# A two-layer diffusion trunk on one core: the FFN's first product by seven block products, on single-bank PSUM tiles

## Chip, core and metric

The kernel runs on one core of a Trainium2 chip. The metric is device microseconds of one execution; three runs of the kernel before give a median of 2444.55 us (2443.7 to 2446.66).

## What is computed

640 tokens (512 latent and 128 context, 1024 wide) pass two layers. All arrays are float32.

```
x = x + g1 * mixers(rmsnorm(x) * (1 + sc1) + sh1)        # three attention branches, gates, output projection
h = rmsnorm(x) * (1 + sc2) + sh2
a, b = split(h @ w_ffn_in)                               # 1024 -> 2 x 2816
x = x + g2 * ((silu(a) * b) @ w_ffn_out)                 # 2816 -> 1024
sh1, sc1, g1, sh2, sc2, g2 = silu(c) @ w_mod + b_mod     # two conditioning vectors c
```

## The kernel before

Activations lie transposed, 128 channels on the partitions and the 640 tokens along the row, in two halves of 320 (`HALF`). For float32 accuracy each operand is a high part (`whi`, `h[:, 0]`) rounded to the matmul's format and a low part (`wlo`, `h[:, 1]`), and `group` (L420) issues three matmuls of 320 columns per 128x128 weight tile: high by high, high by low, low by high.

Weights come in chunks of 128 x 1024 float32, eight tiles each. `weights` loads a chunk to `raw` (two buffers, DMA queue of SP), ScalarE copies it to `whi` (`hi`), and POOL subtracts to `wlo` (`lo`; for attention chunks a DMA accumulates instead). There are four buffers of `whi` and of `wlo`.

The FFN has 22 inner tiles f of 128 channels, in two parts of 11 (`SEG`, `PARTS`). For each f and half `ffn_in` runs two products (gate and up, eight groups each) into one two-bank tile `S`, and `after` applies silu on ScalarE, multiplies on VectorE (`s<-s,S`), copies the high part on ScalarE and subtracts the low part on VectorE (`act<-s,act`). `ffn_out` then multiplies the part's tiles into eight output rows m, each with both halves in an `S` tile, and `residual` adds them to `x` on VectorE (`x<-S`). In the last part the final two rows are done first for one half and then for the other (`FO_SPLIT = 66`).

`mod_dve` makes the conditioning values on VectorE: pieces of `w_mod` (`mr`, 128x512) are multiplied with the two vectors silu(c), spread over all partitions in SBUF (`cb`), and summed along the row (L519, output `md`). In layer 0, 96 of these 320 operations run about the output projection and 224 in the FFN.

The order of all engines is made when the kernel is built: each piece of work is a generator with a priority, and `_Order.run` places the one that can start first by a table of costs (`dve`, `act`, `ptt`, `dma`). Dense products have priority 1000, weights 20, FFN finishing 40, `mod_dve` 200 (lower numbers go first). `MOD_SPREAD = 1.4` is the cost in us by which conditioning products are placed in the FFN. On the chip every engine runs its list in that order.

## Time and profile before

| | us |
|---|---|
| median of 3 runs | 2444.55 |
| profiled execution | 2444.26 |
| its span, first to last instruction | 2442.5 |
| TensorE busy | 2365.4 |
| VectorE busy | 1510.9 |
| ScalarE busy | 1195.5 |
| POOL busy | 773.6 |

The span is that of the profiled execution, and 1.8 us of its time lie around it. PE is TensorE, PEld its weight loads, DVE VectorE, ACT ScalarE. Instructions of helpers carry the helper's line: L311 is ScalarE's activation, L334 and L338 VectorE's two- and three-operand operations, L350 POOL's subtraction, L419 to L421 the three matmuls of a group.

### The profile page before, as it was taken

How to read it: one execution, taken by the hardware profiler on the slowest of the kernel's cores; microseconds unless marked ns; L12 is line 12 of the kernel's file. 1: busy time of each engine (PE TensorE's matmuls, PEld its weight loads, DVE VectorE, ACT ScalarE, POOL GpSimd, SP SyncE). 2: the span in 40 equal slices, each digit the busy share in tenths (PEclk: the TensorE clock that was granted, in tenths of full speed). 3: DMA queues.
4: the chain of work that ended last, by engine and by line, in shares of the span. 5: the costliest groups of instructions: out<-in, count | busy, mean ns of one | idle time of the engine just before them, and what ended most of it. 6: DMA issues, size and time to landing. Idle time of an engine off the chain costs nothing.

```text
span 2442.5 us, 44315 instructions
## 1 busy us (share of the span) xinstructions
PE 2365.4 (97%) x17084; PEld 2322.6 (95%) x17084; DVE 1510.9 (62%) x3621; ACT 1195.5 (49%) x2676; POOL 773.6 (32%) x694
## 2 busy tenths in 40 slices
...
GB/s 238 96 82 114 85 70 64 107 96 100 221 224 112 177 144 142 138 149 149 148 126 113 109 108 101 56 69 109 105 96 142 111 76 70 83 73 78 70 78 61
DMA packets 100579, 274.22 MB, mean 112 GB/s; under 512 B 11408, under 2 KB 25360, under 8 KB 100112
## 3 DMA queue, kind: packets, MB, share of 16 engines
...
## 4 chain that ended last, share of the span: by engine, by line
PE 77%; DVE 8%; issue 3%; DMA 2%; ACT 2%; POOL 1%; DVEq 0%; SPq 0%; POOLq 0%; ACTq 0%
PE S L420 13%; PE S L419 13%; PE S L421 13%; PE B L419 6%; PE B L421 6%; PE B L420 6%; PE B L1028 4%; PE B L722 2%; PE B L723 2%; PE B L724 2%; PE S L1000 2%; PE S L999 2%; PE B L1264 2%; PE B L1263 2%; DVE md L519 1%
## 5 line engine op out<-in xcount | busy, mean ns | idle before, releaser
L350 POOL TENSOR_TENSOR wlo<-raw,whi 128x1024 fp32r<-128x1024 f32 x158 | 390.2, 2471 | 694.1 <-ACT whi L311 693.8
L420 PE MATMUL S<-h,whi 128*128 128x320 f32 x1408 | 438.3, 311 | 6.7 <-DVE h L338 5.8
L419 PE MATMUL S<-h,whi 128*128 128x320 f32 x1408 | 438.2, 311 | 0.0
L421 PE MATMUL S<-h,wlo 128*128 128x320 f32 x1408 | 437.1, 310 | 0.0
L311 ACT ACTIVATE whi<-raw 128x1024 fp32r<-128x1024 f32 x268 | 282.7, 1055 | 282.4 <-PE S L420 229.2
L722 PE MATMUL B<-whi,h 128*128 128x256 f32 x928 | 274.3, 296 | 1.5 <-ACT nat L311 1.5
L420 PEld LDWEIGHTS S<-h,whi 128*128 128x128 f32 x1408 | 266.0, 189 | 9.7 <-DVE h L338 7.0
L723 PE MATMUL B<-wlo,h 128*128 128x256 f32 x928 | 263.2, 284 | 5.0 <-DMA wlo<-raw 5.0
L419 PEld LDWEIGHTS S<-h,whi 128*128 128x128 f32 x1408 | 266.1, 189 | 0.8 <-ACT h L311 0.4
L421 PEld LDWEIGHTS S<-h,wlo 128*128 128x128 f32 x1408 | 266.2, 189 | 0.0
L724 PE MATMUL B<-whi,h 128*128 128x256 f32 x928 | 263.4, 284 | 2.2 <-POOL h L350 2.2
L519 DVE SCALAR_TENSOR_TENSOR md<-mr,cb 128x512 f32<-128x512 f32 x320 | 247.0, 772 | 20.8 <-DMA mr<-wt 16.0
L419 PE MATMUL B<-h,whi 128*128 128x320 f32 x768 | 245.1, 319 | 0.2 <-ACT acc L311 0.2
L421 PE MATMUL B<-h,wlo 128*128 128x320 f32 x768 | 238.2, 310 | 0.7 <-DMA wlo<-raw 0.7
L420 PE MATMUL B<-h,whi 128*128 128x320 f32 x768 | 237.8, 310 | 0.0
L419 PE MATMUL S<-act,whi 128*128 128x320 f32 x704 | 218.0, 310 | 0.0
L421 PE MATMUL S<-act,wlo 128*128 128x320 f32 x704 | 217.5, 309 | 0.0
L420 PE MATMUL S<-act,whi 128*128 128x320 f32 x704 | 217.5, 309 | 0.0
L334 DVE TENSOR_TENSOR s<-s,S 128x320 f32<-128x320 f32 x88 | 42.9, 487 | 281.9 <-ACT s L311 281.8
L419 PE MATMUL B<-u,whi 128*128 128x320 f32 x640 | 202.5, 316 | 5.3 <-ACT u L311 4.2
L311 ACT ACTIVATE s<-S 128x320 f32<-128x320 f32 x88 | 38.5, 438 | 333.1 <-PE S L421 333.1
L311 ACT ACTIVATE P<-S,mx 128x768 f32<-128x768 f32 (+4 forms) x240 | 180.8, 756 | 41.8 <-DVE mx L1013 29.9
...
## 6 DMA issues: line engine op xcount, KB each, us to landing
...
mr<-wt SPq DMA_DIRECT2D x160, 256.0 KB, 3.1
...
```

Of the source, the lines that this page charges most:

```text
L311: fn = lambda: self.nc.scalar.activation(out, in_, func, **kw)
L350: return ("POOL", 0.147 + 0.0021 * _n(out), lambda: self.nc.gpsimd.tensor_tensor(out, a, b, op=op), 0.08)
L419: mm(out, lhsT=wh, rhs=xh, start=first, stop=False)
L420: mm(out, lhsT=wh, rhs=xl, start=False, stop=False)
L421: mm(out, lhsT=wl, rhs=xh, start=False, stop=last)
L519: yield ("DVE", each, lambda w=d["raw"], b=b, r=r: nc.vector.scalar_tensor_tensor(md, w, 1.0, b, op0=ALU.mult, op1=ALU.mult, accum_out=r), ...
L722: mm(d, lhsT=hh, rhs=wh, start=kt == 0, stop=False)
L723: mm(d, lhsT=hh, rhs=wl, start=False, stop=False)
L724: mm(d, lhsT=hl, rhs=wh, start=False, stop=kt == KT - 1)
L999: mm(o, lhsT=q, rhs=kh, start=True, stop=False)
L1000: mm(o, lhsT=q, rhs=kl, start=False, stop=True)
L1028: nc.tensor.transpose(t[:, i * P:(i + 1) * P], a, self.ident)
```

## The change

For inner tiles 3 to 21 (`PLAIN = 3`) the product [gate; up] = W h is taken as a 2 x 2 block product: gate and up are the block rows, the two halves of the 1024 input channels the inner blocks, the two token halves the block columns. Seven block products of four groups replace the eight.

- Inputs: `seven_inputs` makes once per layer, from `h`, four pairs of tiles `ht` (sums and differences of channel and token halves, again high and low). The sums are on VectorE, in `act` buffers.
- Weights: a tile's gate and up chunks come as one unit (`raw`, `raw2`); `sums` makes four 128x512 sums on VectorE (`ws`, and in place in `raw2`), and the unit is split in four high and low parts, three of 1024 and one of 512 columns.
- Outputs: `seven` sends each product to a bank, and `post` combines them with seven additions on VectorE (`fu`, `fv` and in the banks) and a copy on ScalarE. The multiplication with silu now writes into the bank, and the low part is taken from there (`hidden`).
- Banks: the FFN uses six single-bank tiles in turn, four `F` in the place of the `S` tiles and two of the `B` banks.
- Parts of 8, 8 and 6 inner tiles, so three rounds of `ffn_out` a layer.
- Conditioning: silu(c) lies in PSUM (in `S` about the output projection, in two `B` banks in the FFN, half of it at a time there, reloaded between), loaded in pieces through `cr`. `MOD_SPREAD` is 0.75, `mr` has four buffers throughout (before three, in the FFN eight), and the last four conditioning tiles of layer 1 move from layer 0's FFN to layer 1's, so 192 products are in layer 0's and 32 in layer 1's.

```diff
-WO_SPLIT, FO_SPLIT = 4, 66
-SEG = 11
+WO_SPLIT, FO_SPLIT = 4, 6
+SEG = 8
 PARTS = [range(a, min(a + SEG, NF)) for a in range(0, NF, SEG)]
+PLAIN = 3
...
-MOD_SOON, MOD_SPREAD = 0.7, 1.4
+MOD_SOON, MOD_SPREAD = 0.7, 0.75
...
+    def open_banks(self):
+        self.banks = [self.t("F", [P, 512])[:, 0:HALF] for _ in range(4)]
+        for _ in range(2):
+            self.banks.append((yield from self.get("D", [P, 512]))[:, 0:HALF])
...
+        def sums():
+            for c in todo:
+                if not c["seven"]:
+                    continue
+                yield self.wait(c["loaded2"])
+                ws = c["ws"] = yield from self.get("ws", [P, CH])
+                ra, rb = c["raw"], c["raw2"]
+                yield self.tt(ws[:, h1], rb[:, h1], rb[:, h2], ALU.add)
+                yield self.tt(ws[:, h2], ws[:, h1], ra[:, h1], ALU.subtract)
+                self.o.fire(c["s1"])
+                yield self.tt(rb[:, h1], ra[:, h1], rb[:, h1], ALU.subtract)
+                self.o.fire(c["s3"])
+                yield self.wait(c["lo_ok"][1])
+                yield self.tt(ws[:, h2], ra[:, h2], ws[:, h2], ALU.subtract)
+                self.rel("raw")
+                self.o.fire(c["s4"])
...
+                for n, e in enumerate(("loaded", "s1", "s4", "s3") if c["seven"] else ("loaded",)):
+                    yield ("acq", "whi")
+                    yield ("acq", "wlo")
+                    c["hi"].append(self.t("whi", [P, CH], F32R))
+                    c["lo"].append(self.t("wlo", [P, CH], F32R))
+                    yield self.wait(c[e])
+                    x, w = self.part(c, n)
+                    yield self.act(c["hi"][n][:, 0:w], x, AF.Copy)
...
+        n = 512 if home == "T" else D
...
+        def vectors():
+            for _ in range(2):
+                cv.append((yield from self.get(home, [P, n])))
+            used = None
+            for at, _, ok, done in plan:
+                if used is not None:
+                    yield self.wait(used)
+                for c in range(2):
+                    for i in range(2) if at is None else (at,):
+                        r = yield from self.get("cr", [P, 512])
+                        yield self.dma(r, self.I["cb"][:, c, i * 512:(i + 1) * 512], 128 * 4 * 512)
+                        to = 0 if at is not None else i * 512
+                        yield self.act(cv[c][:, to:to + 512], r, AF.Silu)
+                        self.rel("cr")
+                self.o.fire(ok)
+                used = done
...
+                        o = 0 if at is not None else i * 512
+                        b, r = cv[c][:, o:o + 512], a[:, q, c, i:i + 1]
+                        yield ("DVE", each, lambda w=d["raw"], b=b, r=r: nc.vector.scalar_tensor_tensor(
+                            md, w, 1.0, b, op0=ALU.mult, op1=ALU.mult, accum_out=r), 0.13)
...
-            yield self.tt(s, s, d[:, 1], ALU.mult)
-            self.rel("S")
-            yield self.act(act[f][:, 0, half], s, AF.Copy)
-            yield self.tt(act[f][:, 1, half], s, act[f][:, 0, half].bitcast(F32), ALU.subtract)
-            self.rel("s")
-            hit()
-        a, b = part[0], part[1]
-        steps = [(a, 0), (b, 0), (a, 1), (b, 1)] + [(f, half) for f in part[2:] for half in range(2)]
+            yield self.act(s, d[0], AF.Silu)
+            self.bank_done(d[0])
+            yield from self.hidden(s, d[1], act[f][:, :, half], hit)
...
+        for f in part:
+            if f >= PLAIN:
+                act[f] = yield from self.get("act", [P, 2, 2, HALF], F32R)
+                yield from self.seven(h, act[f], act_ok[f])
...
+    def seven_inputs(self, h, h_ok):
...
+            for kt in (k, k2):
+                for half in range(2):
+                    yield self.wait(h_ok[half][kt])
+            t = (yield from self.get("act", [P, 2, 2, HALF], F32R)).rearrange("p a b t -> p a (b t)").bitcast(F32)
+            x, y = t[:, 0], t[:, 1]
+            for kt, z in ((k, x), (k2, y)):
+                yield self.tt(z, h[kt][:, 0].bitcast(F32), h[kt][:, 1].bitcast(F32), ALU.add)
+            yield self.tt(x[:, a], x[:, b], x[:, a], ALU.subtract)
+            yield self.tt(x[:, b], y[:, b], x[:, b], ALU.subtract)
+            yield self.tt(y[:, b], y[:, b], x[:, a], ALU.subtract)
+            yield self.tt(y[:, a], y[:, a], y[:, b], ALU.subtract)
+            hits = self.counter(2, lambda k=k: (self.rel("act"), self.o.fire(self.ht_ok[k])))
...
+                yield self.act(d[:, 0], z, AF.Copy)
+                yield self.tt(d[:, 1], z, d[:, 0].bitcast(F32), ALU.subtract)
+                hits()
...
+    def seven(self, h, act, act_ok):
...
+        def post():
+            s_ok = [self.ev(), self.ev()]
+            yield self.wait(done[1])
+            v = yield from self.get("fv", [P, HALF])
+            yield self.act(v, p[1], AF.Copy)
+            self.bank_done(p[1])
+            yield self.wait(done[6])
+            u = yield from self.get("fu", [P, HALF])
+            yield add(u, p[6], v)
+            self.bank_done(p[6])
+            yield self.wait(done[2])
+            yield add(p[2], p[2], v)
+            o.spawn(gate(0, p[2], s_ok[0]), 39)
+            yield self.wait(done[5])
+            yield add(v, p[5], u)
+            yield self.wait(done[7])
+            yield add(u, p[7], u)
+            self.bank_done(p[7])
+            yield add(p[5], p[5], u)
+            yield self.wait(done[3])
+            yield add(p[3], p[3], v)
+            self.rel("fv")
+            o.spawn(gate(1, p[3], s_ok[1]), 39)
+            def second():
+                yield self.wait(s_ok[1])
+                yield from self.hidden(silu[1], p[5], act[:, :, 1], hit)
+            o.spawn(second(), 40)
+            yield self.wait(done[4])
+            yield add(p[4], p[4], u)
+            self.rel("fu")
+            yield self.wait(s_ok[0])
+            yield from self.hidden(silu[0], p[4], act[:, :, 0], hit)
+        o.spawn(post(), 40)
...
+        def go(i, part, col, xs):
+            p[i] = yield from self.bank()
+            yield self.wait(c["lo_ok"][part])
+            for k in range(n):
+                wh, wl = (t[part][:, col + k * P:col + (k + 1) * P] for t in (c["hi"], c["lo"]))
+                xh, xl = xs(k)
+                yield self.group(p[i], wh, wl, xh, xl, k == 0, k == n - 1)
+            o.fire(done[i])
+        two = lambda t, s: (t[:, 0, s], t[:, 1, s])
+        half = CH // 2
+        yield from go(1, 0, 0, lambda k: two(h[k], a))
+        for ok in self.ht_ok:
+            yield self.wait(ok)
+        yield from go(6, 1, half, lambda k: two(self.ht[k][1], b))
+        yield from go(2, 0, half, lambda k: two(h[n + k], a))
+        self.chunk_done()
+        yield from go(5, 1, 0, lambda k: two(self.ht[k][0], a))
+        self.chunk_done()
+        yield from go(7, 3, 0, lambda k: two(self.ht[k][0], b))
+        yield from go(3, 2, 0, lambda k: two(h[n + k], b))
+        self.chunk_done()
+        yield from go(4, 3, half, lambda k: two(self.ht[k][1], a))
+        self.chunk_done()
+    def hidden(self, s, d, out, hit):
+        yield self.tt(d, d, s, ALU.mult)
+        self.rel("s")
+        yield self.act(out[:, 0], d, AF.Copy)
+        yield self.tt(out[:, 1], d, out[:, 0].bitcast(F32), ALU.subtract)
+        self.bank_done(d)
+        hit()
...
-        split = FO_SPLIT if end else KT * n
+        split = (FO_SPLIT if end else KT) * n
...
-            mods = {"cb": 1, "md": 1, "ma": 2, "mr": 3}
+            mods = {"cr": 1, "md": 1, "ma": 1, "mr": 4}
...
-            fctx = self.pool("f", {"act": SEG, "s": 1})
+            self.scores_ctx.close()
+            pctx = self.pool("pf", {"F": 4}, space=PSUM)
+            fctx = self.pool("f", {"act": SEG, "s": 2, "ht": 8, "raw2": 2, "ws": 1, "fu": 1, "fv": 1})
             o.fire(f_open)
+            o.fire(self.f_ok[l])
+            o.spawn(self.seven_inputs(*h2), 12)
...
+            mctx = self.pool("m", mods)
+            here, ahead = [(l, j) for j in range(20, 24)], [(l + 1, j) for j in range(20)]
+            steps = [((0,), here), ((1,), here)]
             if not last:
-                mctx = self.pool("m", dict(mods, mr=8))
-                here = [(l, j) for j in range(20, 24)] if l == 0 else []
-                self.mod_dve(here + [(l + 1, j) for j in range(24)], 200, MOD_SPREAD)
+                steps += [((1,), ahead), ((0,), ahead)]
+            self.mod_dve(steps, 200, MOD_SPREAD, "T")
```

On VectorE, in layer 0's FFN while inner tiles are computed, the order before was as follows (`md` are conditioning products, `s` and `act` the finishing of inner tiles).

```order
L334 TENSOR_TENSOR act_10764<-s_10901,act_10764 128x320
L519 SCALAR_TENSOR_TENSOR md_10577,ma_10941<-mr_10703,cb_10502 128x512
L519 SCALAR_TENSOR_TENSOR md_10577,ma_10941<-mr_10727,cb_10502 128x512
L334 TENSOR_TENSOR s_10977<-s_10977,S_10905 128x320
L519 SCALAR_TENSOR_TENSOR md_10577,ma_10941<-mr_10727,cb_10502 128x512
L334 TENSOR_TENSOR act_10904<-s_10977,act_10904 128x320
```

At the same place it now reads (`ws` and the row with `raw` on the left are weight sums, `F` and `B` banks, `fu` and `fv` combinations):

```order
L359 TENSOR_TENSOR ws_10976<-raw_1997_10851 128x512
L359 TENSOR_TENSOR act_10817<-F_10285,act_10817 128x320
L359 TENSOR_TENSOR ws_10976<-ws_10976,raw_10773 128x512
L359 TENSOR_TENSOR act_10817<-B_10287,act_10817 128x320
L359 TENSOR_TENSOR raw_1997_10851<-raw_10773,raw_1997_10851 128x512
L359 TENSOR_TENSOR fu_11002<-F_10284,fv_10980 128x320
L617 SCALAR_TENSOR_TENSOR md_10508,ma_10509<-mr_10845,B_10505 128x512
L359 TENSOR_TENSOR B_10286<-B_10286,fv_10980 128x320
L617 SCALAR_TENSOR_TENSOR md_10508,ma_10509<-mr_10902,B_10504 128x512
L359 TENSOR_TENSOR fv_10980<-F_10282,fu_11002 128x320
```

The finishing and the conditioning products read a bank; the weight sums, which are new, stand between them with both inputs in SBUF.

On POOL, one inner tile's low parts were two of 1024 columns and are now these four (the fifth row begins the next tile):

```order
L375 TENSOR_TENSOR wlo_11019<-raw_10773,whi_11018 128x1024
L375 TENSOR_TENSOR wlo_11040<-ws_10976,whi_11039 128x1024
L375 TENSOR_TENSOR wlo_11079<-ws_10976,whi_11078 128x512
L375 TENSOR_TENSOR wlo_11111<-raw_1997_10851,whi_11110 128x1024
L375 TENSOR_TENSOR wlo_11163<-raw_10956,whi_11162 128x1024
```

The second and the third wait for weight sums of VectorE, and the fourth stands behind them.

On VectorE again, the end of layer 0's input transformation, before tile 3's second product (`act_10729` is the fourth pair's sums, `ht` the low parts of transformed inputs):

```order
L359 TENSOR_TENSOR act_10729<-h_10117 128x640
L359 TENSOR_TENSOR ht_10727<-act_10643,ht_10727 128x640
L359 TENSOR_TENSOR act_10729<-h_10121 128x640
L359 TENSOR_TENSOR ht_10728<-act_10643,ht_10728 128x640
L359 TENSOR_TENSOR act_10729<-act_10729 128x320
L359 TENSOR_TENSOR ws_10651<-raw_10603,ws_10651 128x512
L359 TENSOR_TENSOR act_10729<-act_10729 128x320
L359 TENSOR_TENSOR F_10285<-F_10285,s_10743 128x320
```

All of this is new there; weight sums and the finishing of the first three tiles stand among it.

## Rows read from the trace of the kernel before

**Rows 1.** The page, part 1: busy us, share of the span, instructions.
```profile
PE 2365.4 (97%) x17084; PEld 2322.6 (95%) x17084; DVE 1510.9 (62%) x3621; ACT 1195.5 (49%) x2676; POOL 773.6 (32%) x694
```
**Rows 2.** Windows, both FFNs: us, busy PE, PEld, DVE, ACT, POOL; clock, DMA, GB/s.
```profile
767.00:1242.00 475.00, 471.11 (x3183) 468.49 (x3181) 316.06 (x723) 134.70 (x215) 166.59 (x73) 0.99 0.43 145
1955.00:2430.00 475.00, 469.70 (x3165) 467.31 (x3165) 139.83 (x202) 124.19 (x202) 159.92 (x71) 0.99 0.20 71
```
**Rows 3.** Timeline of PE at the FFN's end: start, us, instruction.
```profile
2409.70 0.31 PE L419 MATMUL S<-act,whi 128*128 128x320 f32 x1
...
2419.38 0.31 PE L419 MATMUL S<-act,whi 128*128 128x320 f32 x1
```
**Rows 4.** Groups by form, DVE, layer 0's FFN (767 to 1242 us).
```profile
L519 DVE SCALAR_TENSOR_TENSOR md<-mr,cb 128x512 f32<-128x512 f32 x224 | 170.0, 759 | 3.6
L334 DVE TENSOR_TENSOR act<-s,act 128x320 fp32r<-128x320 f32 x44 | 66.0, 1500 | 4.6 <-ACT act L311 4.5
...
L338 DVE SCALAR_TENSOR_TENSOR x<-S,mo,x 128x320 f32<-128x320 f32 x16 | 8.8, 551 | 51.3 <-PE S L421 51.3
```
**Rows 5.** Tile views of s and md, whole run: ns min/median/max, starts.
```profile
L334 DVE TENSOR_TENSOR s<-s,S x88: 480/487/489, 784.0 to 2350.5; 128x320 f32<-128x320 f32 x88
...
L334 DVE TENSOR_TENSOR act<-s,act x88: 476/1470/2699, 788.7 to 2351.8; 128x320 fp32r<-128x320 f32 x88
...
L519 DVE SCALAR_TENSOR_TENSOR md<-mr,cb x320: 675/686/2935, 623.7 to 1227.6; 128x512 f32<-128x512 f32 x160
```
**Rows 6.** Timeline of DVE, layer 0's norm and FFN.
```profile
761.03 0.48 DVE L334 TENSOR_TENSOR ssq<-ssq,sq 128x320 f32<-128x320 f32 x1
761.43 0.55 DVE L338 SCALAR_TENSOR_TENSOR nu<-x,ac,ssq 128x320 f32<-128x320 f32 x1
...
805.87 2.51 DVE L334 TENSOR_TENSOR act<-s,act 128x320 fp32r<-128x320 f32 x1 [0.21 <-ACT act L311]
808.31 2.90 DVE L519 SCALAR_TENSOR_TENSOR md<-mr,cb 128x512 f32<-128x512 f32 x1
...
811.25 0.69 DVE L519 SCALAR_TENSOR_TENSOR md<-mr,cb 128x512 f32<-128x512 f32 x1
...
811.98 0.69 DVE L519 SCALAR_TENSOR_TENSOR md<-mr,cb 128x512 f32<-128x512 f32 x1
```
**Rows 7.** Timeline of POOL, start of layer 0's FFN.
```profile
794.58 2.41 POOL L350 TENSOR_TENSOR wlo<-raw,whi 128x1024 fp32r<-128x1024 f32 x1 [5.93 <-ACT whi L311]
...
805.61 5.04 POOL L350 TENSOR_TENSOR wlo<-raw,whi 128x1024 fp32r<-128x1024 f32 x2 [4.61 <-ACT whi L311]
815.70 2.76 POOL L350 TENSOR_TENSOR wlo<-raw,whi 128x1024 fp32r<-128x1024 f32 x1 [5.04 <-ACT whi L311]
```
**Rows 8.** Groups by form, POOL and ACT, layer 0's FFN.
```profile
L350 POOL TENSOR_TENSOR wlo<-raw,whi 128x1024 fp32r<-128x1024 f32 x64 | 160.7, 2512 | 272.8 <-ACT whi L311 272.7
...
L311 ACT ACTIVATE whi<-raw 128x1024 fp32r<-128x1024 f32 x67 | 70.8, 1056 | 124.0 <-PE S L420 116.0 <-issue 7.1 <-DMA raw<-w 1.0
```
**Rows 9.** Timeline of DVE: the norm's end, the third tile's end.
```profile
789.13 1.26 DVE L338 SCALAR_TENSOR_TENSOR h<-nu,mo,h 128x192 fp32r<-128x192 f32 x4
...
818.65 0.49 DVE L334 TENSOR_TENSOR s<-s,S 128x320 f32<-128x320 f32 x1 [0.17 <-ACT s L311]
```
**Rows 10.** Window after TensorE's wait at the start of layer 0's FFN.
```profile
776.00:780.00 4.00, 4.00 (x14) 3.38 (x13) 3.82 (x6) 1.00 (x2) 1.43 (x1) 0.50 0.39 134
```
**Rows 11.** Timeline of DVE and a window, end of layer 0's FFN.
```profile
1230.90 0.55 DVE L338 SCALAR_TENSOR_TENSOR x<-S,mo,x 128x320 f32<-128x320 f32 x1 [2.19 <-PE S L421]
...
1241.11 0.68 DVE L338 SCALAR_TENSOR_TENSOR x<-S,mo,x 128x192 f32<-128x192 f32 x2
...
1242.00:1246.00 4.00, 2.32 (x12) 1.64 (x11) 3.96 (x9) 2.61 (x6) 2.41 (x3) 1.00 0.82 205
```
**Rows 12.** Window and DVE group by form, layer 0's output projection (640 to 755, 767 us).
```profile
640.00:755.00 115.00, 104.57 (x683) 103.02 (x682) 99.04 (x259) 35.01 (x57) 25.65 (x14) 0.97 0.72 215
...
L519 DVE SCALAR_TENSOR_TENSOR md<-mr,cb 128x512 f32<-128x512 f32 x84 | 68.7, 818 | 13.2 <-DMA mr<-wt 12.2
```

207 lines of the change are left out of this document (138 added, 69 removed).

## Prediction, made before the change ran

> **What bounds the kernel now.** I read the page first: the span is 2442.5 us, and TensorE is busy for 97% of it, with its weight loads close behind; VectorE comes next at 62% [rows 1]. So the time is TensorE's work, and a change is worth what it takes off TensorE, less what it makes TensorE wait for. The windows then show where the change acts: the FFN runs from 767 to 1242 us in layer 0 and from 1955 to 2430 us in layer 1, TensorE is busy for 471 and 470 of the 475 us, at a granted clock of 0.99 [rows 2]. There is nearly no wait to win there; what can go is matmuls. In the timeline 22 groups of three FFN matmuls lie between 2409.70 and 2419.38 us [rows 3], which gives 9.68 / 66 = 0.1467 us per matmul (the 0.31 us of a row is its length in the pipe). In the same windows VectorE is at 316 us in layer 0 and 140 us in layer 1 [rows 2]: layer 0 carries 224 conditioning products (`md`) in its FFN [rows 4], layer 1 none.
>
> The next view is VectorE against POOL. An operation on VectorE with both inputs in SBUF is sometimes 0.48 us and sometimes 2.5: `act<-s,act` has a minimum of 476, a median of 1470 and a maximum of 2699 ns, while `s<-s,S`, the same shape with one input in PSUM, stays between 480 and 489 in all 88 cases [rows 5]. The timeline shows why: at 805.87 `act<-s,act` takes 2.51 us and at 808.31 an `md` takes 2.90, while POOL has two `wlo` of 2.5 us each from 805.61 on [rows 6, 7]. So POOL holds VectorE up for as long as its own instruction lasts, but only where VectorE reads two tensors from SBUF.
>
> The Trainium skill, page "SBUF — State Buffer", section "SBUF: two separate sides", says this as a rule: VectorE with two SBUF inputs and a GpSimd instruction that reads SBUF hold a shared port pair exclusively, and whichever starts second waits out the whole of the other. By that rule the trace agrees (2.51 against 0.48 us), and the rule speaks against this change, which adds such operations; rival C is what it comes to.
>
> **The change, part by part.** The sum is made against the profiled execution, 2444.3 us; the median of the three runs, 2444.55, is 0.3 us from it.
>
> Matmuls. An inner tile now takes 2 x 2 x 8 groups of three, 96 matmuls or 14.1 us. By seven products of four groups it is 84, or 12.3 us. The order shows 16706 rows on PE before and 16250 now, 456 fewer, which is 12 x 19 tiles x 2 layers. 456 x 0.1467 = **-66.9 us**, half of it in each layer. Everything else is what may be given back.
>
> VectorE inside a block tile. The order shows per tile four weight sums 512 wide with both inputs in SBUF, seven combinations and four finishing operations 320 wide with an input or output in PSUM, and in layer 0 about six conditioning products (some 115 of its 192 stand among the 19 block tiles). A 320-wide operation follows the next after 0.40 us (761.03 to 761.43), a conditioning product after 0.73 (811.25 to 811.98) [rows 6]; a 512-wide sum is then some 0.64 by its width. Layer 0: 4 x 0.64 + 11 x 0.40 + 6 x 0.73 = 11.4 us of the 12.3 us that TensorE has for the tile. It fits, with 0.9 us to spare, before any wait for POOL. Layer 1: 7.0 of 12.3.
>
> POOL has four low parts per tile, three of 1024 and one of 512 columns: 3 x 2.51 + 1.26 = 8.8 us of 12.3 [rows 8], so it is busy 72% of the time in which the sums must run. The conditioning products now read PSUM and are free of it. Bounds for the wait per tile: 0 if the sums fall into POOL's pauses; 4 x 1.0 = 4.0 us if each pays what `act<-s,act` pays on average (1500 ns in this window against a minimum of 476 [rows 4, 5]). I take 2.0: the first sum starts as POOL ends the short low part and begins the next long one, the last starts when POOL waits for it. 11.4 + 2.0 = 13.4 against 12.3, so VectorE is late by 1.1 us more on each tile, and since its order is fixed TensorE ends up waiting for banks and weights: 1.1 x 19 = **+20 us** in layer 0 (0 to 59). In layer 1 7.0 + 4.0 still fits; I put **+4** for single late sums (0 to 15).
>
> ScalarE has 3.5 x 1.056 us of high parts per tile [rows 8] and about 2.5 us more, some 6 of 12.3: covered. Banks: the product held longest is the fourth, from 7.0 us into the tile until its gated result is split, some 1.3 us into the next; by hand at most four of the six banks are held at once, so they cost nothing until VectorE is two products (3.5 us) behind. The weights' second part gets its buffers 7.0 us into the tile before, is split by about 11.4 (1.06 on ScalarE, POOL free from 9.0, 2.5 there) and used at 14.1, 2.7 us later. These two reserves are the cover; the lateness above eats them.
>
> Entry. The second product of tile 3 needs all transformed inputs. Before, the third tile ends at about 818 us (its `s<-s,S` at 818.65) and the norm's last write on VectorE at 790.4 [rows 9]; the tile's first product gives 1.8 us more, so the inputs are due at 819.7. From 790.4 VectorE has 16 operations 640 wide (0.80 by width) and 16 of 320, 9 finishing ones, 4 sums and 3 conditioning products: 12.8 + 6.4 + 3.6 + 2.6 + 2.2 = 27.6, less two that stand before the norm's end: 816.4. Nearly all of it reads two SBUF tensors, and five `wlo` lie between 794.58 and 818.46 [rows 7], 12.6 us in all. With half of them in the way: 822.7, a stall of 3 us, and after a stall TensorE shows the low clock for a while: 14 matmuls in 4 us at a granted 0.50 from 776 on [rows 10], that is 1.2 instead of 2.4 GHz. **+4 us** per layer, **+8** (0 to 24).
>
> Ends. The last two output rows are done by halves; with 6 inner tiles in the last part instead of 11 the first half's end lies 12 groups (5.3 us) ahead of the second's, not 22 (9.7; the rows show 1230.90 and 1241.11). The next layer's norm and the final one start 4.4 us later against TensorE's end. At 1242 TensorE is already half idle, 2.32 of 4 us [rows 11]. **+5 us** over both ends (0 to 10).
>
> Output projection of layer 0. Its conditioning products take 818 ns there against 675 at best [rows 5, 12], and TensorE idles 10 of 115 us with VectorE at 99 [rows 12]. Out of POOL's way they free 84 x 0.14 = 12 us of VectorE, but the DMAs are at 0.72 too, and they stay: **-2 us** (-8 to +4, as the vectors now come by four loads through one buffer).
>
> The third output part adds 16 residual additions a layer on VectorE, 0.55 us each [rows 4], in stretches with six conditioning products per 7 us; they fit, at nothing, and if VectorE is behind there they lengthen the 20 by up to 9.
>
> Sum: -66.9 + 20 + 4 + 8 + 5 - 2 = -31.9, so **2412 us**.
>
> **The rivals.**
> A, VectorE keeps up. The sums fall into POOL's pauses, the wait stays below the 0.9 us to spare, and only small losses stand: -66.9 + 2 (entry) + 2 + 4 - 2 = -61, 2383 us. For it: the finishing operations are moved off two SBUF inputs, and 72% is not all. Against it: 0.9 us is little, and every row class with two SBUF inputs shows waits.
>
> C, VectorE becomes the bound of layer 0 and the kernel is slower. Place: the sums and the entry; price: each sum waits 1.0 us, 11.4 + 4.0 = 15.4 against 12.3, 3.1 x 19 = 59; the entry meets all five low parts, 829 against 819.7, and 3 us of low clock, 24 for both layers; layer 1 15, ends 10: -66.9 + 108 = +41, 2485 us. It turns against the old kernel where the wait per tile passes 0.9 + (66.9 - 15) / 19 = 3.6 us. For it: after a POOL instruction the next one can begin before VectorE's (808.31 is such a row [rows 6]); against it: that needs all four sums to meet POOL every time.
>
> D, both cancel within 0.2%, about what a measurement of this kernel can tell from no change (5 us): a wait of 3.3 to 3.9 us per tile, 2439 to 2449 us.
>
> **How the numbers follow.** The forecast, a gain of which layer 0 gives most of its half back, 0.57; A 0.20; D 0.07; C 0.16. Faster is forecast and A, 0.77; same D, 0.07; slower C, 0.16. The likeliest time is 2412, its own range 2390 to 2439. For 8 in 10 the range reaches down to A's value, 2384, and up over D into the lower part of C, 2454.
>
> **What would show it.** Right: 456 fewer matmuls; layer 1's FFN shorter by 25 us or more, layer 0's by about 10; VectorE above 90% in layer 0's block tiles, sums with a mean of 1 us or more against 0.6, `md` near 690 ns without long ones; one TensorE wait of a few us in tile 3 of each layer. Wrong: if layer 0's FFN shrinks as much as layer 1's (A), if it is longer than 475 us (C), if TensorE's waits in block tiles end by DMA or ScalarE instead of VectorE, or if the entry stalls by over 12 us a layer.

## The result, and the profile after

The changed kernel takes 2433.44 us (median of 4 runs, 2430.18 to 2435.53) beside 2445.14 us for the kernel before in the same comparison: a ratio of 0.9947, 95% interval 0.9933 to 0.996. It is faster by 11.7 us, half a per cent; 32 were forecast. The profiled execution took 2430.18 us, its span is 2428.4 us, 14.1 us less than that of the profile before.

The page's first part and the windows of the two FFN stages, after (columns as in [rows 1, 2]):

```profile
PE 2318.7 (95%) x16628; PEld 2267.0 (93%) x16628; DVE 1783.1 (73%) x4151; ACT 1275.4 (53%) x2818; POOL 916.3 (38%) x770
```
```profile
762.00:1239.00 477.00, 447.07 (x2947) 437.82 (x2945) 430.85 (x909) 172.41 (x281) 236.63 (x111) 0.98 0.41 137
1958.00:2413.00 455.00, 442.09 (x2945) 437.68 (x2943) 298.87 (x535) 165.09 (x270) 234.01 (x108) 0.98 0.25 85
```

TensorE has 456 matmuls less, as forecast. Layer 1's FFN is 20 us shorter than in [rows 2]; layer 0's is as long as it was. There TensorE is idle for 30 of 477 us instead of 4 of 475, and VectorE is busy for 431 us instead of 316.

Where the time went, from the starts of the matmuls in the timeline. A tile's loss is the interval between its first matmul and the next tile's, less its number of matmuls x 0.1467 us; a stage is told from its first matmul to its last:

| us | before | after | difference |
|---|---|---|---|
| start of layer 0's FFN | 767.1 | 762.1 | -5.0 |
| layer 0's FFN | 473.6 | 476.5 | +2.9 |
| from one FFN to the other | 712.6 | 719.4 | +6.8 |
| layer 1's FFN | 474.3 | 454.4 | -19.9 |
| behind it, to the end of the span | 14.8 | 16.0 | +1.2 |

| loss after, us | layer 0 | layer 1 |
|---|---|---|
| inner tile 0 (before: 8.6, 9.3) | 10.0 | 8.2 |
| first block tile, 3 | 6.6 | 7.0 |
| end of part 0: tile 7 and its second product | 3.5 + 4.0 | 3.5 + 4.0 |
| parts 1 and 2 | 20.8 | 0 |
| last second product | 0.5 | 0.5 |

All other tiles run back to back. What I had not expected is the third row: the same 7.5 us in both layers, although layer 1 was to have VectorE time to spare.

VectorE's groups by form in layer 0's FFN (762 to 1239 us) show what changed there:

```profile
L617 DVE SCALAR_TENSOR_TENSOR md<-mr,B 128x512 f32<-128x512 f32 x192 | 130.4, 679 | 2.3
L359 DVE TENSOR_TENSOR ws<-raw 128x512 f32<-128x512 f32 x19 | 41.4, 2180 | 2.3 <-DMA raw<-w 1.4 <-POOL wlo L375 0.9
L359 DVE TENSOR_TENSOR ws<-ws,raw 128x512 f32<-128x512 f32 x19 | 29.2, 1535 | 0.0
L359 DVE TENSOR_TENSOR ma<-ma 128x4 f32<-128x4 f32 x24 | 22.7, 946 | 0.5
L359 DVE TENSOR_TENSOR raw<-raw,raw 128x512 f32<-128x512 f32 x19 | 17.0, 895 | 0.0
...
L359 DVE TENSOR_TENSOR mo<-ma,sm 128x4 f32<-128x4 f32 x24 | 14.6, 608 | 0.5
...
L359 DVE TENSOR_TENSOR ws<-raw,ws 128x512 f32<-128x512 f32 x19 | 13.0, 685 | 2.3 <-POOL wlo L375 2.1
```

The conditioning products with a PSUM input are now even (the tile view has 668/677/692 ns as minimum, median and maximum over both layers' FFN, beside 675/686/2935 in [rows 5]). The weight sums wait for POOL: a 128x512 sum takes 0.68 us where nothing is in its way, and the first two take 2.18 and 1.54 on average. And so do two groups of four elements per partition, `ma` and `mo`, which finish a conditioning tile (they add up its partial sums and the bias): 48 of them take 37.3 us. I had left them out of the sum. The timelines of VectorE and of POOL at the end of part 0 show it:

```profile
869.52 2.34 DVE L359 TENSOR_TENSOR ma<-ma 128x4 f32<-128x4 f32 x1
871.89 0.16 DVE L359 TENSOR_TENSOR mo<-ma,sm 128x4 f32<-128x4 f32 x1
...
877.40 2.35 DVE L359 TENSOR_TENSOR ma<-ma 128x4 f32<-128x4 f32 x1
879.78 2.31 DVE L359 TENSOR_TENSOR mo<-ma,sm 128x4 f32<-128x4 f32 x1
882.01 0.88 DVE L359 TENSOR_TENSOR act<-B,act 128x320 fp32r<-128x320 f32 x2
```
```profile
869.43 2.41 POOL L375 TENSOR_TENSOR wlo<-ws,whi 128x1024 fp32r<-128x1024 f32 x1 [2.51 <-ACT whi L336]
876.08 1.29 POOL L375 TENSOR_TENSOR wlo<-ws,whi 128x512 fp32r<-128x512 f32 x1 [4.24 <-ACT whi L336]
877.35 4.72 POOL L375 TENSOR_TENSOR wlo<-raw,whi 128x1024 fp32r<-128x1024 f32 x2
```

An operation of 0.15 us that starts as POOL does takes 2.34. At 877.40 two in a row wait for two low parts in a row, and `act<-B,act` behind them starts at 882.01, some 4 us after its input was there (ScalarE's copy of it begins at 877.49). That operation frees the bank for which TensorE waits 1.0 us at 882.55, the third row of the waits below. In both layers the four conditioning tiles j = 20 to 23 end there. TensorE's waits in that stretch (872 to 902 us), and its windows at the entry into the block products and there:

```profile
PE F L491 <- ACT act L336: 1.8, 1, 1.8
PE F L493 <- POOL wlo L375: 1.1, 1, 1.1
PE B L491 <- DVE act L359: 1.0, 1, 1.0
PE F L491 <- ACT s L336: 0.6, 1, 0.6
```
```profile
818.00:830.00 12.00, 8.33 (x41) 8.10 (x42) 11.53 (x23) 6.23 (x10) 7.28 (x4) 0.72 0.34 108
872.00:902.00 30.00, 25.33 (x155) 24.05 (x154) 29.76 (x63) 9.48 (x15) 14.85 (x7) 0.94 0.40 137
```

The clock of 0.72 and 0.94 is the mean of a stretch at full speed and one at half (1.2 of 2.4 GHz): the granted clock is 0.50 from 820 to 826.5 us, behind the two waits at the entry, and again from 895 to 898.4, behind the wait of 1.8 us at 894.29. So part of these losses is paid at half clock afterwards. The two waits at the entry end when the transformed inputs `ht` are there:

```profile
819.30 0.41 PE L491 MATMUL F<-ht,whi 128*128 128x320 f32 x1 [1.63 <-ACT ht L336]
822.09 0.64 PE L492 MATMUL F<-ht,whi 128*128 128x320 f32 x1 [2.37 <-DVE ht L359]
```

In layer 0's parts 1 and 2 the granted clock stays at 1.00, and the loss is waiting alone. TensorE's largest waits there (946 to 1239 us), and the window of part 1's inner tiles:

```profile
PE F L493 <- POOL wlo L375: 6.7, 5, 1.5
PE B L493 <- POOL wlo L375: 6.6, 5, 1.6
```
```profile
946.50:1054.50 108.00, 100.70 (x670) 98.08 (x670) 104.59 (x206) 42.88 (x70) 66.16 (x30) 1.00 0.38 124
```

TensorE waits for POOL's low parts of the weights. Three of a tile's four are made from VectorE's sums, and VectorE is busy for 97% of that stretch.

Theory A, from here on: VectorE's operations with two SBUF inputs, the smallest included, wait for POOL's low parts, and VectorE is late by that. The rivals are that the banks or the parts lose time by themselves (B), or that it is the plain number of conditioning products (C). From here on, and in the expectations, the letters are the experiments' own and not those of the prediction's rivals; D to G are explained where they come up.

### The profile page after: what moved, and what is told of

The parts are those of the page before. It is cut to its first block, busy times and chain, and to the rows that moved or that the text cites. A ratio compares the mean times of both kernels' runs of the same rounds, so it can differ in the third digit from the quotient of the medians.

```text
span 2428.4 us, 44516 instructions
## 1 busy us (share of the span) xinstructions
PE 2318.7 (95%) x16628; PEld 2267.0 (93%) x16628; DVE 1783.1 (73%) x4151; ACT 1275.4 (53%) x2818; POOL 916.3 (38%) x770
## 3 DMA queue, kind: packets, MB, share of 16 engines
q0 software_dynamic: 15840, 57.68, 12.4%
## 4 chain that ended last, share of the span: by engine, by line
PE 64%; DVE 18%; issue 5%; POOL 2%; ACT 2%; DMA 2%; DVEq 0%; SPq 0%; POOLq 0%; ACTq 0%
PE B L491 9%; PE B L493 9%; PE B L492 9%; PE F L492 5%; PE F L491 5%; PE F L493 5%; PE B L1127 4%; DVE md L617 3%; PE B L821 3%; PE B L823 3%; PE B L822 3%; PE S L1099 2%; PE S L1098 2%; PE B L1363 2%; PE B L1362 2%
## 5 line engine op out<-in xcount | busy, mean ns | idle before, releaser
L491 PE MATMUL B<-h,whi 128*128 128x320 f32 x956 | 303.5, 317 | 2.6 <-DVE act L359 2.1
L492 PE MATMUL B<-h,whi 128*128 128x320 f32 x956 | 295.6, 309 | 0.0
L493 PE MATMUL B<-u,wlo 128*128 128x320 f32 x640 | 198.7, 310 | 5.2 <-DMA wlo<-raw 5.2
L491 PE MATMUL B<-u,whi 128*128 128x320 f32 x640 | 202.5, 316 | 0.9 <-DVE acc L363 0.7
L375 POOL TENSOR_TENSOR wlo<-ws,whi 128x1024 fp32r<-128x1024 f32 x76 | 141.7, 1864 | 161.0 <-ACT whi L336 152.9
L1112 DVE TENSOR_REDUCE mx<-S 128x1 f32<-128x768 f32 (+4 forms) x240 | 181.8, 765 | 26.3 <-PE S L1099 23.8
L492 PE MATMUL B<-u,whi 128*128 128x320 f32 x640 | 198.5, 310 | 0.0
L823 PEld LDWEIGHTS B<-whi,h 128*128 128x128 f32 x928 | 179.6, 194 | 5.0 <-POOL h L375 3.8
L491 PEld LDWEIGHTS B<-h,whi 128*128 128x128 f32 x956 | 180.2, 189 | 3.8 <-DVE act L359 2.6
L821 PEld LDWEIGHTS B<-whi,h 128*128 128x128 f32 x928 | 179.9, 194 | 3.6 <-issue 1.3
L493 PEld LDWEIGHTS B<-h,wlo 128*128 128x128 f32 x956 | 179.8, 188 | 1.4 <-DMA wlo<-raw 1.4
L492 PEld LDWEIGHTS B<-h,whi 128*128 128x128 f32 x956 | 180.4, 189 | 0.0
L822 PEld LDWEIGHTS B<-wlo,h 128*128 128x128 f32 x928 | 180.3, 194 | 0.0
L359 DVE TENSOR_TENSOR PT<-B,PT 128x512 fp32r<-128x512 f32 (+2 forms) x264 | 154.9, 608 | 20.6 <-ACT PT L336 18.1
```

Source lines behind the costliest of these rows:

```text
L359: return self.dve(_n(out), lambda: self.nc.vector.tensor_tensor(out, a, b, op=op))
L375: return ("POOL", 0.147 + 0.0021 * _n(out), lambda: self.nc.gpsimd.tensor_tensor(out, a, b, op=op), 0.08)
L491: mm(out, lhsT=wh, rhs=xh, start=first, stop=False)
L492: mm(out, lhsT=wh, rhs=xl, start=False, stop=False)
L493: mm(out, lhsT=wl, rhs=xh, start=False, stop=last)
L821: mm(d, lhsT=hh, rhs=wh, start=kt == 0, stop=False)
```

## Experiments

Times are medians beside the kernel before on the same chip. The planner makes a new order for every edit, and the start of layer 0's FFN alone lay between 760.4 and 774.7 us in kernels without another reason for it; so an edit to the FFN is read from its stage's length, and totals that differ by less than some 5 us tell little.

| run | total us (ratio, interval) | FFN 0 | between | FFN 1 | loss of tile 3; end of part 0; parts 1, 2 in layer 0 |
|---|---|---|---|---|---|
| changed kernel | 2433.4 (0.9933 to 0.996) | 476.5 | 719.4 | 454.4 | 6.6; 7.5; 20.8 |
| no_mods_in_ffn | 2397.2 (0.9782 to 0.9809) | 449.6 | 718.7 | 447.8 | 1.9; 1.6; 0 |
| one_input_finish | 2410.6 (0.9839 to 0.9869) | 460.6 | 719.5 | 446.0 | 6.6; 0; 12.6 |
| later_mods | 2438.0 (0.995 to 0.9975) | 469.1 | 729.0 | 456.0 | 6.6; 7.5; 13.1 |
| no_block_products | 2453.1 (1.0017 to 1.0037) | 475.2 | 720.9 | 473.3 | none |
| two_ws_ffn_only | 2399.7 (0.9795 to 0.9828) | 450.2 | 718.7 | 447.3 | 6.2; 0; 2.3 |
| two_ws_old_finish | 2417.5 (0.9869 to 0.9897) | 465.3 | 719.1 | 449.1 | 6.2; 2.3; 11.3 (and 3.7 in the last product) |
| two_ws_spread_plain4 | 2397.2 (0.978 to 0.9814) | 444.3 | 724.8 | 443.1 | 0 (tiles 4 to 7: 0.7); 0; 0.6 |

**Without the FFN's conditioning** (`here` and `ahead` fire at once, the columns are constants):

```diff
-            self.mod_dve(steps, 200, MOD_SPREAD, "T")
+            for k, j in here + ([] if last else ahead):
+                o.fire(self.mod_ok[k][j])
...
```


> The changed kernel with every conditioning product of the two FFN stages left out (the columns keep a constant; the out-projection's 96 products stay). Theory A (VectorE is late because its conditioning work, the small finishing operations included, stands among operations that wait for POOL's low parts): the losses at the end of part 0 (7.5 us in each layer) and those of layer 0's parts 1 and 2 (20.8 us) go, the entry into the first block product (6.6 and 7.0 us) stays: 2433.4 - 15 - 20.8 = about 2398 us. Rival B (the end of a part loses time by itself, by the six banks or by the chain of POOL's low parts): only the 20.8 us go, about 2413 us, and the last inner tile of part 0 still loses 3 to 4 us in layer 1.

2397.2 us. The second product of part 0 and all of parts 1 and 2 lose nothing, in either layer: theory A's number, and not B's. The run leaves out the products together with their finish, so it does not tell A from C; the next one does. One thing neither theory said: the entry's loss did not stay in tile 3 but spread over tiles 3 to 7 (1.9, 1.1, 1.9, 1.6, 1.6 us in layer 0).

**The finish with one input** (a third column of `ma` holds the bias, put there by ScalarE; `ac` and `gh` go to ScalarE too):

```diff
-                        yield self.tt(a[:, :, :, 0], a[:, :, :, 0], a[:, :, :, 1], ALU.add)
-                        yield from self.mod_finish(l, j, a[:, :, :, 0])
+                        yield from self.mod_finish_one(l, j, a)
...
+        yield self.dve(12, lambda: nc.vector.tensor_reduce(out, a, axis=AX.X, op=ALU.add))
```


> The changed kernel with the conditioning's finishing operations (128x4 sums with two SBUF inputs) replaced by one reduction of a single input, which also adds the bias column. Theory A says that such a sum waits 2.3 us for POOL whenever a low part runs: in layer 0's FFN the 24 sums and 24 bias sums took 22.7 + 14.6 us on VectorE and should fall to some 10 in all. The end of part 0 (eight finishing operations in each layer) should lose 3 us or less instead of 7.5, and layer 0's parts 1 and 2 some 8 us less: 2415 to 2425 us, and each reduction below 0.4 us. Rival C (it is the 0.68 us products by their number, and the small operations fit into idle time): within 3 us of the changed kernel, 2430 to 2434 us.

2410.6 us, 23 us less. VectorE's group by form in layer 0's FFN:

```profile
L692 DVE TENSOR_REDUCE mo<-ma 128x4 f32<-128x12 f32 x24 | 3.9, 160 | 0.4
```

37.3 us have become 3.9, the end of part 0 loses nothing in either layer, and layer 0's parts 1 and 2 lose 12.6 instead of 20.8. The number of conditioning products is unchanged, so C is out as the cause of part 0's end, and of the 8.2 us that parts 1 and 2 gained. The Trainium skill, page "SBUF — State Buffer", section "Who interferes with whom", says that a `tensor_reduce` on this chip never contends for the shared pair; the trace agrees: no reduction took over 0.17 us. The Trainium skill, page "VectorE: DVE Perf Modes", section "Rules for kernel authors", calls `tensor_reduce` on a hot path the slowest operation of VectorE and advises to consider restructuring. For one this small beside a busy POOL the measurement says otherwise: 0.16 us where the two sums took 0.95 and 0.61 on average. What a large reduction costs no run here shows.

**Conditioning for layer 1 moved out of layer 0's FFN** (12 of 20 tiles, into layer 1's output projection):

```diff
-            if l == 0:
+            if True:
                 mctx = self.pool("m", mods)
...
-            here, ahead = [(l, j) for j in range(20, 24)], [(l + 1, j) for j in range(20)]
+            here, ahead = [(l, j) for j in range(20, 24)], [(l + 1, j) for j in range(8)]
```


> The changed kernel with 12 of the 20 sets of layer 1's conditioning (96 of the 160 products ahead) moved out of layer 0's FFN into layer 1's out-projection, as layer 0 has them. Both A and C: with 96 of 160 gone, layer 0's parts 1 and 2 lose 5 to 9 us instead of 20.8: minus 12 to 16 us. Layer 1's out-projection gives some of it back if VectorE is late there: 0 to 5 us. Together 2418 to 2426 us. If the losses of layer 0's parts 1 and 2 come from the wait for POOL alone and not from the products' number (rival B), it stays within 3 us of 2433 us.

2438.0 us, a miss: layer 0's FFN gained 7.4 us and the stretch between the FFNs lost 9.6. Part 2 loses nothing any more; part 1 loses 13.1 us instead of 11.3, though the timeline shows only 27 products among its tiles instead of 48. What has moved among its tiles are finishes, which had stood at its end and behind it; C does not explain that. In layer 1's output projection TensorE now waits for weights (window 1860 to 1990 us; after, this row is absent there); that the conditioning's rows crowd them out is argued, not shown:

```profile
PE B L493 <- DMA wlo<-raw: 5.6, 4, 2.2
```

**All of the change but the block products:**

```diff
-PLAIN = 3
+PLAIN = NF
...
-            o.spawn(self.seven_inputs(*h2), 12)
...
```

Two more edits go with it: inner tiles from the third on are taken one by one, and the release of `ht` goes.

> All of the change but its block products: every inner tile by the two plain products, on the six single banks, in parts of 8, 8, 6, with the conditioning vectors in PSUM. If the banks, the parts and PSUM cost nothing by themselves, it takes the time before (2445) less the 5 us that the out-projection gained, plus at most the 7 us that were added between the FFNs and 1 us at the end: 2440 to 2448 us, with no inner tile but the first losing more than 1 us. If the six banks or the third part cost time by themselves (rival B), the ends of the parts lose 3 us or more here too: 2455 us or more.

2453.1 us, 5 us above the range expected without rival B, but not by rival B: no tile but the first loses anything, and the ends of the parts are dense. So the banks and the parts cost nothing. What it has over the kernel before lies between the FFNs, 720.9 us beside 712.6, so the +6.8 us there do not come from the block products. In the changed kernel, with block products or without, with or without the FFN's conditioning, one wait of the same size stands in layer 1's attention (here after, window 1490 to 1550 us; before, from 1494 to 1546, there is only one row, of 1.8 us over three waits):

```profile
PE S L1098 <- ACT P L336: 4.7, 1, 4.7
```
```profile
1491.00:1547.00 56.00, 49.78 (x364) 48.50 (x364) 50.01 (x119) 40.71 (x93) 12.79 (x17) 0.94 0.31 76
```

4.7 us, and some 3 us more by the half clock (0.94 over 56 us). That this is an order of small steps which the planner chose is argued; which line of the change tips it was not tried.

**At the entry, an attempt by order and one by a fourth plain tile** (both on the one-input finish):

```diff
+        if first:
+            yield from go(2, 0, half, lambda k: two(h[n + k], a))
+            self.chunk_done()
         for ok in self.ht_ok:
             yield self.wait(ok)
         yield from go(6, 1, half, lambda k: two(self.ht[k][1], b))
-        yield from go(2, 0, half, lambda k: two(h[n + k], a))
-        self.chunk_done()
+        if not first:
...
```


> The one-reduction finish with the first block tile of each layer in the order 1, 2, 6, 5, 7, 3, 4: its second product needs no transformed input. By theory D the wait at the entry shrinks by one product (12 matmuls, 1.8 us) in each layer, and perhaps the stretch at half clock behind it goes: minus 2 to minus 8 us against the one-reduction finish, 2403 to 2409 us. By rival E (the low parts are late, not the transformed inputs) nothing changes: 2409 to 2412 us.

2417.7 us (0.9869 to 0.991). Tile 3 of layer 0 lost 2.5 us instead of 6.6, but tiles 4 to 7 lost 2.2, 2.9, 1.5 and 1.9. The total is above what either theory expected.

```diff
-PLAIN = 3
+PLAIN = 4
```


> The one-reduction finish with four plain inner tiles instead of three in each layer. Theory D (the first block tile loses 6.6 and 5.5 us because VectorE has not yet made its transformed inputs and first weight sums): another 14 us of plain products hide that; 24 matmuls more in all cost 3.5 us, the first block tile then loses 0 to 2 us: minus 5 to minus 8 us against the one-reduction finish, 2403 to 2406 us. Rival E (the supply of low parts for the first block tiles is the limit wherever they begin): the loss moves to the fourth tile, plus 3.5 us, 2414 us.

2413.3 us (0.9839 to 0.9887). The first block tile, now 4, lost nothing, as theory D had it, but tiles 5, 6 and 7 lost 2.0, 2.0 and 3.6: the loss moved, though not where rival E had it. I read both runs as rival E's limit, the supply of a tile's four low parts: the 6.6 us at tile 3 also give the low parts their lead.

Why they cannot keep up shows in the run without conditioning, where nothing else is in the way. POOL, and then VectorE's sums, between 847 and 862 us:

```profile
847.34 1.31 POOL L375 TENSOR_TENSOR wlo<-ws,whi 128x512 fp32r<-128x512 f32 x1 [1.53 <-ACT whi L336]
848.61 5.24 POOL L375 TENSOR_TENSOR wlo<-raw,whi 128x1024 fp32r<-128x1024 f32 x2
857.37 2.37 POOL L375 TENSOR_TENSOR wlo<-ws,whi 128x1024 fp32r<-128x1024 f32 x1 [3.52 <-ACT whi L336]
```
```profile
848.68 2.89 DVE L359 TENSOR_TENSOR ws<-raw 128x512 f32<-128x512 f32 x1 [0.42 <-POOL wlo L375]
...
851.90 2.50 DVE L359 TENSOR_TENSOR ws<-ws,raw 128x512 f32<-128x512 f32 x1
```

The first sum of the next tile may not begin before POOL has read the one `ws` tile (847.34, the short part). At that moment POOL begins two long parts; both sums wait for them, and POOL then stands idle for 3.5 us until the high part of their result is there. The round takes 13.9 us (the next `wlo<-ws` of 512 columns starts at 861.27) beside TensorE's 12.3. This loop is theory G.

The loop does not cost that much everywhere. In part 1 of the same run the first sum waits as long, but POOL's two long parts stand apart:

```profile
966.90 2.42 POOL L375 TENSOR_TENSOR wlo<-raw,whi 128x1024 fp32r<-128x1024 f32 x1
971.54 2.60 POOL L375 TENSOR_TENSOR wlo<-raw,whi 128x1024 fp32r<-128x1024 f32 x1 [2.23 <-ACT whi L336]
```
```profile
966.98 2.89 DVE L359 TENSOR_TENSOR ws<-raw 128x512 f32<-128x512 f32 x1 [0.33 <-POOL wlo L375]
...
970.19 0.67 DVE L359 TENSOR_TENSOR ws<-ws,raw 128x512 f32<-128x512 f32 x1
```

The second sum then takes 0.67 us, a round takes 12.4, and TensorE loses nothing.

**The conditioning spread out, and part 0's low part by a transfer** (both on the one-input finish):

```diff
-MOD_SOON, MOD_SPREAD = 0.7, 0.75
+MOD_SOON, MOD_SPREAD = 0.7, 1.1
```


> The one-reduction finish with the conditioning's planned cost at 1.1 instead of 0.75: fewer products fall into one inner tile, more beside the second product and in part 2. If the 12.6 us that layer 0's parts 1 and 2 still lose come from the number of conditioning products in an inner tile, they fall to 3 to 8 us: minus 4 to minus 9 us against the one-reduction finish, 2402 to 2407 us. If they come from the block products' own sums, which wait for POOL, nothing changes (2409 to 2412 us).

2417.2 us (0.9862 to 0.9907). Parts 1 and 2 lost 1.7 us in all, with 70 products among their tiles instead of 76, and layer 0's FFN took 451.9 us, 8.8 less than with the one-input finish. But layer 1's norm then waited 12.0 us for the last product (`PE B L843 <- DVE md`), so that the stretch between the FFNs took 731.5 us; the profile, of the slowest of its five runs, also begins layer 0's FFN 9 us later and has layer 1's 4.7 us longer.

```diff
-                    if c["add"]:
+                    if c["add"] or c["seven"] and n == 0:
                         yield self.dma_add(c["lo"][n].bitcast(F32), x)
```


> The one-reduction finish with the low part of each block tile's first weight part made by ScalarE and an accumulating transfer instead of by POOL's 2.3 us subtraction. Theory A: POOL then holds VectorE's two-input operations for some 5.9 us of an inner tile's 12.3 instead of 8.2; the first weight sum should fall from 2.36 us to about 1.7 us and layer 0's parts 1 and 2 should lose 4 to 8 us instead of 12.6: 2403 to 2407 us. Rival F: the transfer lands later than POOL's subtraction did, and TensorE waits for the first low part of every block tile, or POOL's issue of it holds up the other low parts: 2420 us or more.

2478.4 us (1.0109 to 1.0152): rival F. The first weight sum still takes 2.05 us on average in layer 0's FFN, not 1.7. TensorE's waits, whole run:

```profile
PE F L493 <- DMA wlo<-raw: 42.0, 20, 3.3
PE B L493 <- DMA wlo<-raw: 24.6, 12, 3.4
```

**Two `ws` tiles**, first with two row tiles `mr` everywhere, and the entry's order on top of it:

```diff
-            mods = {"cr": 1, "md": 1, "ma": 1, "mr": 4}
+            mods = {"cr": 1, "md": 1, "ma": 1, "mr": 2}
...
-            fctx = self.pool("f", {"act": SEG, "s": 2, "ht": 8, "raw2": 2, "ws": 1, "fu": 1, "fv": 1})
+            fctx = self.pool("f", {"act": SEG, "s": 2, "ht": 8, "raw2": 2, "ws": 2, "fu": 1, "fv": 1})
```


> The one-reduction finish with two weight-sum tiles instead of one, paid for with two conditioning row tiles instead of four. Theory G: behind TensorE's entry, in part 0, the block tiles are held to 13.9 us by a loop: the next tile's first sum needs the one weight-sum tile, which comes free just as POOL begins two low parts in a row; the first two sums then wait for both (2.89 and 2.50 us instead of 0.68), and POOL afterwards idles 3.5 us for the high part of their result. With a second tile the sums can come earlier: the first block tile of each layer should lose 2 to 4 us instead of 6.6 and 5.5, and layer 0's later parts 6 to 10 us instead of 12.6: minus 6 to minus 12 us against the one-reduction finish, 2399 to 2405 us. If the loss is VectorE's volume, not the loop: no change, 2408 to 2414 us; with two row tiles the conditioning products may also wait for their rows, plus 2 to 10 us.

> The same with the first block tile in the order 1, 2, 6, 5, 7, 3, 4. With one weight-sum tile this order cut the first block tile's loss to 2.5 us but the following four lost 1.5 to 2.9 us each. Theory G: with the loop open they lose nothing, so 2 to 5 us less than the kernel with two weight-sum tiles alone. If the low parts' supply has another limit, they still lose 1.5 us or more each: 5 to 8 us more than it.

2411.5 us (0.9847 to 0.9876) and 2413.6 us (0.9855 to 0.9888). Layer 0's FFN took 438.2 and 438.6 us, but they began it at 789.0 and 789.5 us, behind one wait of 22.2 us for the output projection's conditioning, which is late with two row tiles:

```profile
PE F L491 <- DVE md L623: 22.2, 1, 22.2
```

The order brought nothing (layer 1's tile 3 loses 6.6 us with it and 6.7 without); tiles 4 to 7 no longer lost 1.5 us or more each. So in the FFN alone, with four row tiles in the output projection:

```diff
             no.close()
-            mctx = self.pool("m", mods)
+            mctx = self.pool("m", dict(mods, mr=2))
```


> The one-reduction finish with two weight-sum tiles, and two conditioning row tiles in the FFN stages alone; the out-projection keeps four. In the run with two row tiles everywhere layer 0's FFN took 438.2 us beside 460.6 us, but it began 25 us later, behind one wait of 22.2 us for a conditioning product, so that its gain could not be read. Theory G (the loop through the one weight-sum tile): layer 0's FFN begins at 762 to 766 us again, its parts 1 and 2 lose 3 to 6 us instead of 12.6, its entry 3 to 7 us: 2398 to 2405 us. Rival (VectorE only had its lead because the FFN began late): parts 1 and 2 lose 10 us or more again, 2408 to 2413 us.

2399.7 us; parts 1 and 2 of layer 0 lose 2.3 us instead of 12.6, as theory G has it, though the entry keeps its 6.2 and 6.7 us. The edit changes two things: no run has two row tiles and one `ws` tile. A thinner flow of products does not explain the gain, since 81 of them stand among the tiles of parts 1 and 2, and 76 with one `ws` tile; but finish_spread, with one `ws` tile and 70, comes down to 1.7 us too. So the second tile is one way to make VectorE's work fit, and fewer products per tile is another; how much of the gain is the loop alone stays open. VectorE's groups (830 to 1240 us), with one tile (one_input_finish) and with two:

```profile
L359 DVE TENSOR_TENSOR ws<-raw 128x512 f32<-128x512 f32 x17 | 42.3, 2489 | 2.1 <-POOL wlo L375 1.9
```
```profile
L359 DVE TENSOR_TENSOR raw<-raw,raw 128x512 f32<-128x512 f32 x17 | 35.2, 2070 | 0.0
...
L359 DVE TENSOR_TENSOR ws<-raw 128x512 f32<-128x512 f32 x17 | 14.5, 854 | 0.2 <-DMA raw<-w 0.2
```

The waiting for POOL has not gone: most of it has moved from the first sum to the third, whose result is split last of the four. All four sums of these tiles take 85 us instead of 95.

**Two `ws` tiles with the old finish** (the last two edits on the changed kernel itself, without the reduction) tell the two causes apart:

> The changed kernel with two weight-sum tiles in the FFN stages and two conditioning row tiles there, but its old finish (small sums with two inputs). Theory A and G together (small sums wait 2.3 us each, and the loop hands any delay on to TensorE): part 0's end still loses 3 to 8 us in each layer, layer 0's parts 1 and 2 5 to 12 us instead of 20.8: 2412 to 2424 us. If the loop alone is the cause, the finish no longer matters: 2398 to 2404 us, with no loss at part 0's end.

2417.5 us, 18 us more than with the new finish (15.1 and 1.8 of them in the two FFN stages): the finish still matters with two `ws` tiles, and so do the tiles with the new finish. Part 0's end loses 2.3 and 2.7 us instead of 7.5, a little less than expected; parts 1 and 2 of layer 0 lose 11.3.

**The finish in the kernel before.** First everywhere, then in the FFN alone:

```diff
+                    if each == MOD_SPREAD:
+                        yield from self.mod_finish_one(l, j, a)
+                    else:
+                        yield self.tt(a[:, :, :, 0], a[:, :, :, 0], a[:, :, :, 1], ALU.add)
+                        yield from self.mod_finish(l, j, a[:, :, :, 0])
```

> The kernel before with the one-reduction finish. There the small sums took 0.24 us each, since POOL makes low parts for 22 tiles of two and VectorE has 5 us to spare in an inner tile: theory A expects no more than 2 us of gain, 2443 to 2447 us beside 2445 us. If the finish is dear by itself, whatever POOL does, it gains 10 us or more here too.

> The kernel before with the one-reduction finish in the FFN stages alone. In the run with it everywhere the FFN stages took 472.9 and 473.2 us beside 473.6 and 474.3 us, but the planner made the out-projection 18.6 us later and the stretch between the FFNs 9 us longer, which has nothing to do with the question. Theory A: before, VectorE had time to spare and the small sums took 0.24 to 0.27 us: the two FFN stages within 2 us of 473.6 and 474.3 us, and the total within 5 us of 2445 us unless the planner's order between the FFNs shifts. If the finish is dear by itself: the FFN stages 5 us or more shorter.

2471.8 us (1.0091 to 1.0121) and 2458.9 us (1.003 to 1.0064): the totals missed, both ways of thinking had them lower. The FFN stages are as theory A has them, 473.7 and 474.4 us in the second run beside 473.6 and 474.3: without block products the small sums cost the FFN nothing. What was added lies outside it, in a start at 774.7 instead of 767.1 us and in 719.5 instead of 712.6 us between the FFNs, where the planner made another order (in the first run 785.7 and 721.9 us). That a local edit moves the order elsewhere by 7 us and more is the caveat to every total here.

**Which edits add up.** A planned cost of 0.9 on the one-input finish, then with two `ws` tiles in the FFN, then with the fourth plain tile too; and last the two `ws` tiles and the fourth plain tile at 0.75:

```diff
-MOD_SOON, MOD_SPREAD = 0.7, 0.75
+MOD_SOON, MOD_SPREAD = 0.7, 0.9
...
-PLAIN = 3
+PLAIN = 4
```

> The one-reduction finish with the conditioning's planned cost at 0.9. At 1.1 layer 0's parts 1 and 2 lost 1.7 us instead of 12.6, but layer 1's first norm then waited 12 us for the last conditioning product. At 0.9 the products should end before the second product of part 2 does, so that this wait stays away, and parts 1 and 2 should lose 5 to 10 us: minus 2 to minus 7 us against the one-reduction finish, 2403 to 2408 us. If the norm still waits: 2412 us or more.

> The same with the conditioning's planned cost at 0.9. If the loop and the number of products in an inner tile are two separate causes, each cures only part: 2395 to 2402 us, parts 1 and 2 of layer 0 lose less than 3 us. If they are the same (products only matter through the loop): as the kernel without it, within 3 us.

> The same with four plain inner tiles. With one weight-sum tile the entry's loss moved from the first block tile to the third to fifth (2.0, 2.0, 3.6 us). Theory G: with the loop open the low parts keep up, so that the fourth plain tile takes away the 6 to 10 us of the entry for 1.8 us of matmuls in each layer: minus 6 to minus 12 us against the run with three, 2386 to 2395 us. Rival E (the supply of low parts has another limit): within 3 us of it.

> The one-reduction finish, two weight-sum tiles and four plain inner tiles, with the conditioning's planned cost at 0.75 again. At 0.9 the same kernel took 2397 us, its stretch between the FFNs being 724.8 us beside 718.7 us at 0.75. If the three edits add up, the entry's 6.2 and 6.7 us go for 3.5 us of matmuls and the stretch between the FFNs stays at 719 us: 2387 to 2394 us. If the spread is what let four plain tiles work (its products keep out of part 0): 2397 to 2402 us.

2403.4 us (0.9815 to 0.9844), as expected; 2411.6 us (0.984 to 0.9877), against expectation: parts 1 and 2 lose 2.1 us, hardly less than the 2.3 without the spread, and the entry 10.7 and 8.5; 2397.2 us (0.978 to 0.9814), the entry gone; and 2399.3 us (0.9786 to 0.9815), no better than two_ws_ffn_only. At 0.75 (two_ws_plain4) tiles 4 to 7 of layer 1 lose 4.8 us again, so the fourth plain tile works fully only with the spread, and between the FFNs the kernel with the spread takes 6 us more (724.8 beside 718.8). The best kernels take 2397 to 2400 us, 2% less than the kernel before, some 35 us less than the change as made; among the three no difference can be told.

## Why the prediction was wrong

The direction was right, and so was the largest term. The step that failed is a term put at nothing: the sums that finish a conditioning tile. They are in none of the prediction's sums, and they cost 15 us at the ends of part 0, where 4 were allowed for layer 1 and none for layer 0. That is 11 of the 17.8 us by which the sum was too good. Term by term:

- **Matmuls, -66.9**: 456 fewer, as said.
- **VectorE late in layer 0, +20**: 20.8 us, in parts 1 and 2. That the size came out is luck in part. VectorE was over TensorE's 12.3 us a tile and TensorE waited for weights, as said, but 8.2 of the 20.8 us went with the new finish, which had not been priced. For the other 12.6 the wait of 2.0 us per tile was of the right kind and a little small: the four sums take 2.18, 1.54, 0.90 and 0.69 us, 2.7 more than the 2.56 by width. With two `ws` tiles and the new finish 2.3 us are left.
- **Layer 1, +4 "for single late sums"**: 7.5, all at the end of part 0; and **the same 7.5 in layer 0, not in the sum at all**. I priced operations with two SBUF inputs by their width and left out the 128x4 sums, which took 0.23 to 0.27 us on average before. But each can cost what POOL's instruction still has to run, and POOL is busy for some 8.4 of a block tile's 12.3 us (2.41 + 1.29 + 4.72 in the rows above). The kernel before already showed it, in the maximum of its tile view:

```profile
L334 DVE TENSOR_TENSOR ma<-ma x40: 149/162/2293, 632.8 to 1228.3; 128x4 f32<-128x4 f32 x40
```

The rule of the Trainium skill that I had cited (page "SBUF — State Buffer", section "SBUF: two separate sides") has no width in it either; the trace agrees with it down to four elements (0.15 us alone, 2.38 at worst). The change also moves 32 products and their finish into layer 1's part 0, and the sum gives layer 1's VectorE no conditioning at all. The single `ws` tile has a part in these 15 us: with two, the old finish loses 2.3 and 2.7 us there.
- **Entry, +8**: 13.6. The transformed inputs were late, and almost when said: the last wait for them ends at 822.09 us where 822.7 was worked out. But TensorE waits 4.0 us in layer 0 and not 3, and the stretch at half clock behind it, from 820 to 826.5 us, brings the loss to 6.6 where 1 was put for the clock. The loop through `ws` did not add to these 13.6: with two `ws` tiles 6.2 and 6.7 are left. It shows in later tiles once the entry is shorter.
- **Ends, +5**: 1.2 at the end. Between the FFNs 6.8 were added, but in the attention, by the planner's order, which I had no term for.
- **Output projection, -2**: -5.0 at the start of the FFN, inside the bounds given, but that start moves by more than this between orders of the planner.
- **Banks, at nothing**: right, as the run without block products shows.

Sum: -66.9 + 20.8 + 15.0 + 13.6 + 6.8 + 1.2 - 5.0 + 0.3 (tile 0) = -14.2 beside -14.1 of the two profiles. The measured time lies in the forecast's own range, 2390 to 2439, but near its upper end. Of the prediction's rivals, A is refuted, D's 2439 to 2449 was not reached, and C has the place right in layer 0 at a third of its price, but not the verdict.

Of its signs, 456 matmuls, VectorE above 90%, the slow sums and the even `md` came true. Layer 1's FFN is shorter by 19.9 us, not 25, and layer 0's is 2.9 us longer, not 10 shorter. One sign of being wrong came true: layer 0's FFN is longer than 475 us, though the kernel as a whole is faster. TensorE's waits in parts 1 and 2 of layer 0 end by POOL for 13.3 of 15.4 us, which the signs name on neither side.
